# Seven half-depth block products instead of eight in three chunks of a feed-forward

## The chip, the core and the metric

The kernel runs on one core of a Trainium2 chip. The core has a matrix unit (TensorE, PE in the profile, with its weight loads as PEld), VectorE (DVE), ScalarE (ACT), GpSimd (POOL), a queue engine that only starts transfers (SyncE, SP), an on-chip memory of 128 partitions (SBUF) and eight banks of accumulators (PSUM), each 128 x 512 float32. The metric is device time in microseconds, the median of several runs.

## The reference

One block of a streaming encoder on x (256 rows x 2048), all in float32:

```python
h = modulate(rms_norm(x, ffn1_pre_g[l]), sh1, sc1)
y = swiglu(h, ffn1_w_gu[l], ffn1_w_down[l])
x = x + 0.5 * gt1 * rms_norm(y, ffn1_post_g[l])
...
x = x + gt2 * rms_norm(y, mix_post_g[l])
h = modulate(rms_norm(x, ffn2_pre_g[l]), sh3, sc3)
y = swiglu(h, ffn2_w_gu[l], ffn2_w_down[l])
x = x + 0.5 * gt3 * rms_norm(y, ffn2_post_g[l])
```

where `swiglu(h, w_gu, w_down)` is `(silu(h @ G) * (h @ U)) @ w_down`, with G and U the two halves of w_gu, each 2048 x 5504. Between the two feed-forwards lie an in-projection, attention, a spatial gate and an out-projection. The modulation vectors (sh, sc, gt) are a product of silu(c) with a 2048 x 18432 matrix. The change touches the gate and up products of the second feed-forward.

## The kernel before

**Products.** A float32 product is made of three matmuls: every operand is split into a high part (rounded to the matrix unit's type) and a low part (the rest), and `mm3` (L111) multiplies high by high, high by low and low by high into one bank. Weights arrive by transfers of 1 MB into `raw` tiles (three buffers, `load`, L117), and `split` (L152) makes the parts, 1024 columns at a time: ScalarE copies to the high part (L155), VectorE subtracts (L156). The parts go to buffers that `slot` (L143) takes from a repeating sequence of pools; in the second feed-forward these are 3 of `wx3` and 4 of `wsp`, seven pairs in all.

**The feed-forward** (`ffn`, L324). The 5504 columns form eleven chunks: ten of 512 and a last one of 384. `visit` (L342) loads the weights of two k-tiles (gate and up of each), splits them, and does, for two k-tiles, gate and up, and two row tiles of x, one `mm3` each: 24 matmuls of 128 x 512. Eight visits make a chunk, on four PSUM banks from the pool `pmm` (six banks; `ptr` has the other two). `act` (L395) then does silu(gate) on ScalarE and the product with up on VectorE. `trans` (L411) turns the result so that it can be a weight of the next product, half a chunk later, through `ptr`. When two chunks are ready and a third has been computed, `down` (L430) multiplies the two by their rows of w_down: for each of four column blocks two loads, 48 matmuls into two banks, then an addition to y (L453). The last chunk has `down_last` (L455), which also does the norm and the result.

In the second feed-forward the chunks go in order 0 to 10 (L583). Chunk 0 has its own form (`lead_chunk`, L356). The downs come after chunks 2, 4, 6, 8 and 10, for the pairs 0 and 1, 2 and 3, 4 and 5, 6 and 7, 8 and 9.

**Order.** The code is written in program order; a scheduler places the instructions on the engines at compile time and may move one ahead where its operands are ready, and each engine then executes its own list in order. SP issues all weight loads in one list. A load waits there until its buffer is free, and the loads behind it wait too.

**Modulation blocks.** The modulation matrix is worked off in the background: `tick` (L223), called at each visit, adds a rate to a counter and, whenever that passes one, issues `ada_block` (L198), a load of 1 MB into a two-buffer pool `adap` and a 2048-wide multiply-and-sum on VectorE (L202). It also runs one step of the list `later`, if there is one. `flush_ada` (L234) issues what is left of a vector, `gate` (L239) makes the row of gt that the norm needs.

**Around the second feed-forward.** x after mixing (`x2`) is made by `post` (L309), `pre` (L271) turns it into h for the feed-forward, and `finish3` (L1049) adds the result to `x2` and stores it. `x2` stays in SBUF from one to the other. `rstd` (L173) uses a small power on GpSimd (L178).

Of the kernel before, what the change touches and what calls it, by code (L numbers as in the profile page):

```python
# [18 lines left out]
P = 128  # L19
# [10 lines left out]
CHUNKS = [(c, min(CH, FF - c)) for c in range(0, FF, CH)]  # L30
MAX_REL = 128
# [31 lines left out]
def block_kernel(ctx: ExitStack, tc: tile.TileContext, a: dict, out: bass.AP):  # L63
# [21 lines left out]
    x_dram = dr.tile([S, D], F32, tag="x1", name="x1")  # L85
    xp = ctx.enter_context(tc.tile_pool(name="xp", bufs=1))
# [30 lines left out]
    def load(src, off, n):  # L117
        raw = wraw.tile([P, 2048], F32, tag="raw", name=nm("raw"))
        nc.sync.dma_start(raw[:, :n], src[off:off + P * n].rearrange("(p n) -> p n", p=P))
        return raw  # L120
# [203 lines left out]
    def ffn(wgu, wdn, h, avp, ahp, plan, rate, gate_of, finish, lead=(), after_lead=(), ahead=None):  # L324

        hi, lo = h
        C = len(CHUNKS)
# [10 lines left out]
        def gu_load(c, p):  # L338
            off, w = CHUNKS[c]
            return load(wgu, 2 * D * off + p * P * 4 * w, 4 * w)  # L340
# [53 lines left out]

        def act(c):  # L395
            w = CHUNKS[c][1]
            res = []
            for t in range(NT):
                gu = [ps_of[c][b][t][:, :w] for b in range(2)]
                if c in acc:  # L400
                    for b in range(2):
                        nc.vector.tensor_tensor(acc[c][b][t], acc[c][b][t], gu[b], op=ALU.add)
                    gu = [acc[c][b][t] for b in range(2)]
                av = avp.tile([P, CH], F32, tag="av", name=nm("av"), bufs=2)
                nc.scalar.activation(av[:, :w], gu[0], AF.Silu)
                nc.vector.tensor_tensor(av[:, :w], av[:, :w], gu[1], op=ALU.mult)
                res.append(av)
            act_of[c] = res
            del ps_of[c]
# [20 lines left out]
        def down(cs):  # L430
            fresh = not y
            if fresh:
                y.extend(yp.tile([P, D], F32, tag=f"y{t}", name=nm(f"y{t}")) for t in range(NT))
            for n in range(4):
                ns = slice(n * CH, (n + 1) * CH)
                ps = [pmm.tile([P, CH], F32, tag="mm", name=nm("dn")) for _ in range(NT)]
                for c in cs:
                    off, w = CHUNKS[c]
# [145 lines left out]
        tick_acc[1] = rate if plan else 0.0  # L584
        for c in todo:
            if plan and c not in acc and slots["hold"] is not None:
                use_slots((wsp, 4), (slots["hold"], 3))
                slots["hold"] = None
            p0 = max(p for d, p, _ in plan if d == c) + 1 if c in acc else 0
            pm, pe = (p0 + KT // 2) // 2, KT // 2  # L590
            if lead and c == 0:
                lead_chunk(0, lead)
                use_slots(*after_lead)
                p0 = pe
            else:
                ps_of[c] = banks()
            for p in range(p0, pe):
                if p == pm:
# [3 lines left out]
                visit(c, p, p == p0, p == pe - 1)  # L602
            act(c)
            tick_acc[1] = rate
            if c == C - 1:
                g = gate_of()
                tick_acc[1] = 0.0
            if len(ready) == 2:
                down(ready)
# [368 lines left out]
    with tc.tile_pool(name="gp2", bufs=1) as gp:  # L978
# [47 lines left out]
        with tc.high_priority():  # L1026
            for t in range(NT):
                for b in range(2):
                    r = evac_b(t, 2 + b, ps[b][t])
                pre(2, x2, t, post(x2, t, y, r), h3)  # L1030
    mxs.close()
# [3 lines left out]
    with ExitStack() as ahs:  # L1035
# [8 lines left out]

        def gate3():
            flush_ada(GT[2])
            return gate(2, 0.5, gp)

        def finish3(t, y, r):  # L1049
            for j in range(4):  # L1050
                js = slice(j * CH, (j + 1) * CH)
                nc.vector.scalar_tensor_tensor(out=x2[t][:, js], in0=y[t][:, js], scalar=r, in1=x2[t][:, js], op0=ALU.mult, op1=ALU.add)
                nc.sync.dma_start(out[t * P:(t + 1) * P, js], x2[t][:, js])

        ffn(a["w_gu2"], a["w_dn2"], h3, avp, ahp, None, 0.15, gate3, finish3, lead=lead,
            after_lead=((wx3, 3), (wsp, 4)))
# [7 lines left out]
def _gu(w):  # L1064
    g, u = w[:, :FF].reshape(KT, P, FF), w[:, FF:].reshape(KT, P, FF)
    units = []
    for c, n in CHUNKS:
# [64 lines left out]
```

## Time and profile before

| | us |
|---|---|
| median of 3 runs | 1838.58 |
| lowest, highest | 1838.19, 1840.62 |
| the profiled execution | 1839.32 |
| its span, first to last instruction | 1837.2 |

| engine | busy us | share of the span |
|---|---|---|
| PE | 1803.2 | 98% |
| PEld | 1501.1 | 82% |
| DVE | 1328.4 | 72% |
| ACT | 854.5 | 47% |
| POOL | 31.3 | 2% |

The profile is that of one execution. Its page shows the span in 40 slices of some 46 us, with each engine's busy share in tenths; the second feed-forward is in the last 16 of them. Further views group the instructions by line, list them in order of time, list who waited for whom, or give the busy time of each engine in a chosen stretch. Matmuls overlap in the matrix unit, so one lasts longer than the distance to the next, and a busy share of 100% says that there is no hole, not how fast the work goes.

### The profile page before, as it was taken

The numbers are of one execution on the slowest core, as the hardware profiler recorded it, in microseconds if no ns is written. First come the engines' busy times: TensorE is split into PE (matmuls) and PEld (weight loads), VectorE is DVE, ScalarE is ACT, GpSimd is POOL, SyncE is SP. The second block draws the span as 40 slices with busy tenths as digits, with TensorE's granted clock in tenths as the row PEclk, the third lists the DMA queues.
The fourth block names the chain that finished last, engine by engine and source line by source line (L and its number), as shares of the span: only waits on it lengthen the run. The fifth ranks groups of instructions, "written<-read, shape, count | busy, mean of one in ns | idle before, by whom it ended". The sixth has DMA issues, their size and how long they took to land.

```text
span 1837.2 us, 21286 instructions
## 1 busy us (share of the span) xinstructions
PE 1803.2 (98%) x8271; PEld 1501.1 (82%) x8271; DVE 1328.4 (72%) x1481; ACT 854.5 (47%) x1105; POOL 31.3 (2%) x59
## 2 busy tenths in 40 slices
PE   7999999999999999999999999999999999999997
PEld 6777788888888898788888887888888888888896
DVE  7989998988877876768789986774445445445456
ACT  6544354444443344645555557444443443443342
POOL 0000000000000000000001000000000000000000
PEclk9999999999999999999999999999999999999999
DMA  9988788898888876479788974875555555555461
GB/s 395 385 335 318 286 320 342 326 367 332 336 335 321 329 289 261 172 276 358 292 307 326 382 291 165 332 305 187 195 191 187 196 191 187 196 190 186 160 250 70
DMA packets 71477, 499.11 MB, mean 272 GB/s; under 512 B 7968, under 2 KB 8144, under 8 KB 13136
## 3 DMA queue, kind: packets, MB, share of 16 engines
q1 hardware_dynamic: 70560, 492.48, 70.2%
q0 software_dynamic: 720, 5.24, 0.7%
q8 instruction: 65, 1.06, 0.2%
q14 instruction: 36, 0.29, 0.0%
q10 hardware_dynamic: 96, 0.02, 0.0%
HBM read 493.50 MB, written 4.22 MB: 271 GB/s over the span
## 4 chain that ended last, share of the span: by engine, by line
PE 93%; DVE 4%; ACT 1%; issue 1%; DMA 0%; POOL 0%; POOLq 0%; DVEq 0%; SPq 0%; ACTq 0%
PE gu L114 16%; PE gu L115 16%; PE gu L113 16%; PE dn L113 8%; PE dn L114 8%; PE dn L115 8%; PE pj L113 4%; PE pj L115 4%; PE pj L114 4%; PE wo L113 1%; PE wo L115 1%; PE wo L114 1%; DVE lo L156 1%; PE atp L418 1%; PE xtp L281 1%
## 5 line engine op out<-in xcount | busy, mean ns | idle before, releaser
L155 ACT CAST hi<-raw 128x1024 fp32r<-128x1024 f32 (+1 forms) x628 | 645.9, 1042 | 811.5 <-PE gu L115 422.6
L156 DVE TENSOR_TENSOR lo<-raw,hi 128x1024 fp32r<-128x1024 f32 (+1 forms) x628 | 747.8, 1208 | 380.9 <-ACT hi L155 379.5
L113 PE MATMUL gu<-hi,hhi 128*128 128x512 f32 (+1 forms) x1396 | 536.8, 387 | 8.9 <-DVE acc L392 4.2
L114 PE MATMUL gu<-lo,hhi 128*128 128x512 f32 (+1 forms) x1396 | 537.9, 385 | 0.4 <-DVE lo L156 0.3
L115 PE MATMUL gu<-hi,hlo 128*128 128x512 f32 (+1 forms) x1396 | 537.7, 385 | 0.0
L202 DVE CUSTOM_DVE_ANT_0 ada<-ada,c_bc,small 128x2048 f32<-128x2048 f32 x144 | 337.4, 2344 | 9.6 <-PE qkt L797 9.0
L113 PEld LDWEIGHTS gu<-hi,hhi 128*128 128x128 f32 x1396 | 262.4, 188 | 62.4 <-ACT hi L155 5.2
L114 PEld LDWEIGHTS gu<-lo,hhi 128*128 128x128 f32 x1396 | 263.0, 188 | 50.3 <-DVE lo L156 1.2
L115 PEld LDWEIGHTS gu<-hi,hlo 128*128 128x128 f32 x1396 | 262.9, 188 | 50.0
L113 PE MATMUL dn<-hi,ah 128*128 128x512 f32 x640 | 249.2, 389 | 0.0
L114 PE MATMUL dn<-lo,ah 128*128 128x512 f32 x640 | 249.0, 389 | 0.0
L115 PE MATMUL dn<-hi,al 128*128 128x512 f32 x640 | 249.0, 389 | 0.0
L113 PEld LDWEIGHTS dn<-hi,ah 128*128 128x128 f32 x640 | 120.1, 188 | 25.1
L115 PEld LDWEIGHTS dn<-hi,al 128*128 128x128 f32 x640 | 120.1, 188 | 25.0
L114 PEld LDWEIGHTS dn<-lo,ah 128*128 128x128 f32 x640 | 120.2, 188 | 24.8
L113 PE MATMUL pj<-hi,hhi 128*128 128x512 f32 x304 | 120.9, 398 | 0.0
L114 PE MATMUL pj<-lo,hhi 128*128 128x512 f32 x304 | 120.4, 396 | 0.0
L115 PE MATMUL pj<-hi,hlo 128*128 128x512 f32 x304 | 120.1, 395 | 0.0
L115 PEld LDWEIGHTS pj<-hi,hlo 128*128 128x128 f32 x304 | 57.1, 188 | 11.1
L114 PEld LDWEIGHTS pj<-lo,hhi 128*128 128x128 f32 x304 | 57.4, 189 | 10.7
L113 PEld LDWEIGHTS pj<-hi,hhi 128*128 128x128 f32 x304 | 57.4, 189 | 10.6
L453 DVE TENSOR_TENSOR y<-y,dn 128x512 f32<-128x512 f32 x64 | 41.9, 682 | 17.5 <-PE dn L115 17.5
(167 smaller groups left out, 1071.8 us busy)
## 6 DMA issues: line engine op xcount, KB each, us to landing
raw<-in_w_gu_dram SPq DMA_DIRECT2D x158, 1024.0 KB, 4.8
ada<-in_w_ada_dram SPq DMA_DIRECT2D x144, 1024.0 KB, 7.0
raw<-in_w_dn_dram SPq DMA_DIRECT2D x86, 1024.0 KB, 4.8
raw<-in_w_in_dram SPq DMA_DIRECT2D x40, 1024.0 KB, 6.2
raw<-in_w_out_dram SPq DMA_DIRECT2D x16, 1024.0 KB, 7.3
raw<-in_w_gu_dram SPq DMA_DIRECT2D x16, 768.0 KB, 5.3
x<-in_x_dram SPq DMA_DIRECT2D x4, 1024.0 KB, 7.5
gate<-gd POOLq DMA_DIRECT2D x3, 1024.0 KB, 8.4
```

The lines of the kernel that those rows point to most:

```text
L113: nc.tensor.matmul(ps, ah, wh, start=start, stop=False)
L114: nc.tensor.matmul(ps, ah, wl, start=False, stop=False)
L115: nc.tensor.matmul(ps, al, wh, start=False, stop=stop)
L155: i_hi = nc.scalar.copy(hi[:, :n], raw)
L156: i_lo = nc.vector.tensor_tensor(lo[:, :n], raw, hi[:, :n].bitcast(F32), op=ALU.subtract)
L202: inst = nc.vector.tensor_tensor_reduce(out=st, in0=st, in1=c_bc, scale=1.0, scalar=bada[:, i:i + 1], op0=ALU.mult, op1=ALU.add, accum_out ...
L281: nc.tensor.matmul(ps[:, q, :], x[t][:, (4 * j + q) * P:(4 * j + q + 1) * P], dg, start=True, stop=True)
L418: nc.tensor.transpose(ps[:, q, :], av[:, q * P:(q + 1) * P], ident)
L453: nc.vector.tensor_tensor(y[t][:, ns], y[t][:, ns], ps[t], op=ALU.add)
```

## The change

Write h as blocks of 128 rows by 1024 (half the depth), and the weights of a chunk as blocks of 1024 by 512: gate and up, upper and lower half. Then gate and up of both row tiles are a 2 x 2 by 2 x 2 block product, eight block products of half the depth. For the chunks 5, 7 and 9 (`FAST`) the new code forms the same four results out of seven, from sums and differences of blocks on both sides:

- `sum_steps` makes four combinations of the blocks of h, once, before they are needed: two sums that put high and low parts together again, four differences, and their split into parts. They run as steps of `later` during the first down. The results lie in tiles that were those of `x2`, of the broadcast c vector and of the gate row.
- `fast_visit` loads the blocks of one k-tile of a half into a tile of `adap` (four blocks in part 0, three in part 1), adds blocks to each other in place on VectorE (three additions in part 0, one in part 1), splits all of them, and does one `mm3` for each: 12 matmuls in part 0, 9 in part 1. Eight visits make a part.
- Part 0 of chunk c+1 is done between the visits of the down that follows chunk c, one before each. It takes four banks of `pmm`; that down therefore uses `ptr` for every second column block. `first_sums` combines its four results.
- Part 1 is done in the next ordinary chunk, two visits each behind its visits 1 to 4, on three more banks. `second_sums` combines these with the first ones and does the activation. `trans` of the chunk comes behind visit 6, that of the chunk before it moves from visit 4 to visit 1.
- `x2` is stored to DRAM by GpSimd's queue after mixing and loaded again (`x3`) at the last chunk.
- The rate of the modulation blocks in the second feed-forward goes from 0.15 to 0.77.
- The host lays out the weights of the three chunks in the order in which the new visits read them.

```diff
+FAST = (5, 7, 9)
+HK = KT // 2
+def gu_offsets(fast):
+    res, off = [], 0
+    for c, (_, n) in enumerate(CHUNKS):
+        res.append(off)
+        off += HK * P * (2048 + 1536) if c in fast else 2 * D * n
+    return res
...
+    x2_dram = dr.tile([S, D], F32, tag="x2", name="x2")
...
-    def load(src, off, n):
-        raw = wraw.tile([P, 2048], F32, tag="raw", name=nm("raw"))
+    def load(src, off, n, raw=None):
+        if raw is None:
+            raw = wraw.tile([P, 2048], F32, tag="raw", name=nm("raw"))
         nc.sync.dma_start(raw[:, :n], src[off:off + P * n].rearrange("(p n) -> p n", p=P))
...
+        def multiply(gus):
+            res = []
+            for g, u in gus:
+                av = avp.tile([P, CH], F32, tag="av", name=nm("av"), bufs=2)
+                nc.scalar.activation(av, g, AF.Silu)
+                nc.vector.tensor_tensor(av, av, u, op=ALU.mult)
+                res.append(av)
+            return res
+        a_hl = {}
+        def sum_steps():
+            r = []
+            def rows(t):
+                r.append(adap.tile([P, KT, P], F32, tag="ada", name=nm("asum")))
+                ts = slice(t * P, (t + 1) * P)
+                nc.vector.tensor_tensor(r[t], hi[:, :, ts].bitcast(F32), lo[:, :, ts].bitcast(F32), op=ALU.add)
+            def minus(o, a, b):
+                o, a, b = (r[t][:, HK * i:HK * (i + 1), :] for t, i in (o, a, b))
+                nc.vector.tensor_tensor(o, a, b, op=ALU.subtract)
+            def to_hl(t):
+                tiles = sum_tiles(t)
+                for i in range(2):
+                    ks = slice(HK * i, HK * (i + 1))
+                    split_act(r[t][:, ks, :], tiles[0][:, ks, :], tiles[1][:, ks, :])
+                for i, name in enumerate((("a3", "a7"), ("a6", "a1"))[t]):
+                    a_hl[name] = [v[:, HK * i:HK * (i + 1), :] for v in tiles]
+            return [lambda: rows(0), lambda: rows(1),
+                    lambda: minus((0, 0), (0, 1), (0, 0)), lambda: minus((0, 1), (0, 1), (1, 1)),
+                    lambda: minus((1, 1), (1, 1), (0, 0)), lambda: minus((1, 0), (1, 0), (1, 1)),
+                    lambda: to_hl(0), lambda: to_hl(1)]
+        def first_banks():
+            return [pmm.tile([P, CH], F32, tag="mm", name=nm("m")) for _ in range(4)]
+        def second_banks():
+            return [pmm.tile([P, CH], F32, tag="mm", name=nm("m")) for _ in range(2)] + \
+                   [ptr.tile([P, CH], F32, tag="tr", name=nm("m"))]
+        def fast_visit(c, part, p, ps):
+            n = (2048, 1536)[part]
+            raw = load(wgu, offs[c] + part * HK * P * 2048 + p * P * n, n,
+                       adap.tile([P, D], F32, tag="ada", name=nm("raw")))
+            blk = [raw[:, i * CH:(i + 1) * CH] for i in range(n // CH)]
+            sums = ((1, 0), (2, 1), (3, 2)) if part == 0 else ((2, 0),)
+            for i, j in sums:
+                nc.vector.tensor_tensor(blk[i], blk[i], blk[j], op=ALU.add)
+            sp = [split(raw[:, o:min(o + 1024, n)]) for o in range(0, n, 1024)]
+            a = lambda name: [v[:, p, :] for v in a_hl[name]]
+            if part == 0:
+                sts = [a("a3"), hst(p, 0), a("a1"), a("a7")]
+            else:
+                sts = [hst(p, 1), hst(p + HK, 1), a("a6")]
+            for i, st in enumerate(sts):
+                s = slice((i % 2) * CH, (i % 2 + 1) * CH)
+                mm3(ps[i], st, (sp[i // 2][0][:, s], sp[i // 2][1][:, s]), p == 0, p == HK - 1)
+        def spare(i):
+            return sm.tile([P, CH], F32, tag=("xn", "h32")[i], name=nm("cs"), bufs=2)
+        def first_sums(ps):
+            m3, m5, m1, m7 = ps
+            t1, t2, t3 = spare(0), spare(0), spare(1)
+            nc.scalar.copy(t1, m1)
+            nc.scalar.copy(t2, m5)
+            nc.vector.tensor_tensor(t3, t2, m3, op=ALU.add)
+            nc.vector.tensor_tensor(t2, t1, t2, op=ALU.subtract)
+            nc.vector.tensor_tensor(t1, t1, m3, op=ALU.add)
+            nc.vector.tensor_tensor(t2, t2, m7, op=ALU.add)
+            return t1, t2, t3
+        def second_sums(c, ts, ps):
+            m2, m4, m6 = ps
+            t1, t2, t3 = ts
+            t4 = spare(1)
+            nc.scalar.copy(t4, m2)
+            nc.vector.tensor_tensor(t2, t2, m4, op=ALU.add)
+            nc.vector.tensor_tensor(t1, t1, t4, op=ALU.subtract)
+            nc.vector.tensor_tensor(t4, t4, m4, op=ALU.add)
+            nc.vector.tensor_tensor(t1, t1, m6, op=ALU.add)
+            act_of[c] = multiply([(t2, t3), (t4, t1)])
...
-        def down(cs):
-            fresh = not y
+        def down(cs, fill=()):
+            fill = list(fill)
+            fresh, fast_on = not y, bool(fill)
             if fresh:
                 y.extend(yp.tile([P, D], F32, tag=f"y{t}", name=nm(f"y{t}")) for t in range(NT))
             for n in range(4):
                 ns = slice(n * CH, (n + 1) * CH)
-                ps = [pmm.tile([P, CH], F32, tag="mm", name=nm("dn")) for _ in range(NT)]
+                pool, tag = (ptr, "tr") if fast_on and n % 2 else (pmm, "mm")
+                ps = [pool.tile([P, CH], F32, tag=tag, name=nm("dn")) for _ in range(NT)]
                 for c in cs:
+                    if fill:
+                        fill.pop(0)()
...
+        seven = {}
         for c in todo:
+            if c in fast:
+                continue
             if plan and c not in acc and slots["hold"] is not None:
                 use_slots((wsp, 4), (slots["hold"], 3))
                 slots["hold"] = None
...
                 p0 = pe
             else:
                 ps_of[c] = banks()
+            second = c - 1 in fast
             for p in range(p0, pe):
-                if p == pm:
+                if p == (p0 + 1 if second else pm):
                     for r in ready:
                         if r not in stat:
                             trans(r)
                 visit(c, p, p == p0, p == pe - 1)
+                if second and 1 <= p <= 4:
+                    if p == 1:
+                        mb = second_banks()
+                    for i in range(2):
+                        fast_visit(c - 1, 1, 2 * (p - 1) + i, mb)
+                    if p == 4:
+                        second_sums(c - 1, seven.pop(c - 1), mb)
+                        ready.append(c - 1)
+                if second and p == pe - 2:
+                    trans(c - 1)
             act(c)
             tick_acc[1] = rate
+            if fast and c == 2:
+                later.extend(sum_steps())
             if c == C - 1:
                 g = gate_of()
                 tick_acc[1] = 0.0
             if len(ready) == 2:
-                down(ready)
+                if c + 1 in fast:
+                    ma = first_banks()
+                    down(ready, [lambda p=p: fast_visit(c + 1, 0, p, ma) for p in range(HK)])
+                    seven[c + 1] = first_sums(ma)
+                else:
+                    down(ready)
                 ready = []
...
+                nc.gpsimd.dma_start(x2_dram[t * P:(t + 1) * P, :], x2[t])
...
+        def sum_tiles(t):
+            flush_ada(GT[2])
+            pools = (((xp, "x0"), (xp, "x1")), ((const, "c_bc"), (gp, "gate")))[t]
+            return [p.tile([P, KT, P], F32R, tag=tag, name=nm("ahl")) for p, tag in pools]
+        x3 = []
         def gate3():
             flush_ada(GT[2])
+            x3.extend(load_x(x2_dram, nc.gpsimd))
...
-        ffn(a["w_gu2"], a["w_dn2"], h3, avp, ahp, None, 0.15, gate3, finish3, lead=lead,
-            after_lead=((wx3, 3), (wsp, 4)))
+                nc.vector.scalar_tensor_tensor(out=x3[t][:, js], in0=y[t][:, js], scalar=r, in1=x3[t][:, js], op0=ALU.mult, op1=ALU.add)
+                nc.sync.dma_start(out[t * P:(t + 1) * P, js], x3[t][:, js])
+        ffn(a["w_gu2"], a["w_dn2"], h3, avp, ahp, None, 0.77, gate3, finish3, lead=lead,
+            after_lead=((wx3, 3), (wsp, 4)), fast=FAST, sum_tiles=sum_tiles)
...
+    for i, (c, n) in enumerate(CHUNKS):
+        if i in fast:
+            b = lambda v, k: v[k, :, c:c + n]
+            units += [np.stack([b(u, k + HK), b(u, k), b(g, k), b(g, k + HK)], axis=1) for k in range(HK)]
+            units += [np.stack([b(g, k), b(g, k + HK), b(u, k)], axis=1) for k in range(HK)]
+            continue
```

More of the change, by code (lines that the diff above doesn't have):

```diff
@@ L322, in block_kernel, with ffn @@
     LEAD = 8
-    def ffn(wgu, wdn, h, avp, ahp, plan, rate, gate_of, finish, lead=(), after_lead=(), ahead=None):
+    def ffn(wgu, wdn, h, avp, ahp, plan, rate, gate_of, finish, lead=(), after_lead=(), ahead=None,
+            fast=(), sum_tiles=None):
         hi, lo = h
+        offs = gu_offsets(fast)
         C = len(CHUNKS)
@@ L338, in gu_load @@
         def gu_load(c, p):
-            off, w = CHUNKS[c]
-            return load(wgu, 2 * D * off + p * P * 4 * w, 4 * w)
+            w = CHUNKS[c][1]
+            return load(wgu, offs[c] + p * P * 4 * w, 4 * w)
         def visit(c, p, start, stop, bank_outer=False, raw=None, qs=(0, 1), sp=None):
@@ L1051, in finish3, with _gu @@
                 js = slice(j * CH, (j + 1) * CH)
-                nc.vector.scalar_tensor_tensor(out=x2[t][:, js], in0=y[t][:, js], scalar=r, in1=x2[t][:, js], op0=ALU.mult, op1=ALU.add)
-                nc.sync.dma_start(out[t * P:(t + 1) * P, js], x2[t][:, js])
-        ffn(a["w_gu2"], a["w_dn2"], h3, avp, ahp, None, 0.15, gate3, finish3, lead=lead,
-            after_lead=((wx3, 3), (wsp, 4)))
+                nc.vector.scalar_tensor_tensor(out=x3[t][:, js], in0=y[t][:, js], scalar=r, in1=x3[t][:, js], op0=ALU.mult, op1=ALU.add)
+                nc.sync.dma_start(out[t * P:(t + 1) * P, js], x3[t][:, js])
+        ffn(a["w_gu2"], a["w_dn2"], h3, avp, ahp, None, 0.77, gate3, finish3, lead=lead,
+            after_lead=((wx3, 3), (wsp, 4)), fast=FAST, sum_tiles=sum_tiles)
 def _flat(units):
     return np.concatenate([np.ascontiguousarray(u).reshape(-1) for u in units])
-def _gu(w):
+def _gu(w, fast=()):
     g, u = w[:, :FF].reshape(KT, P, FF), w[:, FF:].reshape(KT, P, FF)
     units = []
-    for c, n in CHUNKS:
+    for i, (c, n) in enumerate(CHUNKS):
[4 more added lines that the diff above has]
+            continue
         for k in range(0, KT, 2):
@@ L1117 @@
         "w_out": _flat(_pairs(w["w_out"][0], (0, 8), ((0, 1), (2, 3))) + _pairs(w["w_out"][0], (8, 16), ((0, 1), (2, 3)))),
-        "w_gu2": _gu(w["ffn2_w_gu"][0]),
+        "w_gu2": _gu(w["ffn2_w_gu"][0], FAST),
         "w_dn2": _down(w["ffn2_w_down"][0]),
```

## The prediction

> **What bounds the kernel now.** I read the page first, then the windows of the second feed-forward, the waits in them, and single timelines for durations. The change lies wholly in that last stage, but for two stores just before it.
>
> ```profile
> span 1837.2 us, 21286 instructions
> ...
> PE 1803.2 (98%) x8271; PEld 1501.1 (82%) x8271; DVE 1328.4 (72%) x1481; ACT 854.5 (47%) x1105; POOL 31.3 (2%) x59
> ...
> PE   7999999999999999999999999999999999999997
> ...
> DVE  7989998988877876768789986774445445445456
> ...
> PEclk9999999999999999999999999999999999999999
> ```
>
> The reader is to see that the matrix unit (PE) has no hole between the first and the last slice, that its clock is full throughout, and that VectorE (DVE), at 8 to 9 tenths in the first feed-forward, falls to 4 or 5 in the second. A busy PE may still be one that runs slowly, so I ask for its rate next: the windows, with the columns PE, PEld, DVE, ACT, POOL, clock, DMA share and GB/s.
>
> ```profile
> 1377.10:1420.60 43.50, 43.50 (x193) 36.02 (x192) 24.38 (x24) 17.84 (x19) 0.00 (x0) 1.00 0.54 193
> 1420.60:1465.03 44.43, 44.43 (x202) 36.88 (x201) 22.00 (x20) 17.86 (x19) 0.00 (x0) 1.00 0.52 189
> 1377.10:1509.46 132.36, 132.36 (x594) 109.77 (x593) 68.37 (x64) 54.54 (x57) 0.00 (x0) 1.00 0.53 191
> ```
>
> The cuts are the moments at which ScalarE starts the activation of a finished chunk:
>
> ```profile
> 1332.67 1.08 ACT L405 ACTIVATE av<-gu 128x512 f32<-128x512 f32 x2
> 1377.10 1.08 ACT L405 ACTIVATE av<-gu 128x512 f32<-128x512 f32 x2
> ...
> 1465.03 1.08 ACT L405 ACTIVATE av<-gu 128x512 f32<-128x512 f32 x2
> 1509.46 1.08 ACT L405 ACTIVATE av<-gu 128x512 f32<-128x512 f32 x2
> ```
>
> From 1332.67 to 1377.10 is one gate/up chunk: 16 k-tiles x 2 row tiles x 2 (gate, up) x 3 = 192 matmuls, with 8 small transposes, 44.43 us. From 1377.10 to 1465.03 is one such chunk and one down product of 4 x 2 x 24 = 192 matmuls: 87.93 us. The difference, 43.50 us, is 192 matmuls alone: **0.2266 us for one 128x512 matmul**; the transposes take the other 0.93 us. The round repeats (132.36 us = two chunks and one down).
>
> ```profile
> DVE lo L156 <- ACT hi L155: 65.5, 49, 1.5
> ACT hi L155 <- PE gu L115: 52.9, 33, 1.7
> ACT hi L155 <- PE dn L115: 26.6, 16, 1.7
> ```
>
> These are all the waits of that round. ScalarE waits for PE to give back a split buffer, VectorE waits for ScalarE, PE waits for nobody. So PE's instruction count sets the time, and a removed matmul is worth its whole spacing as long as that stays so.
>
> **The change, part by part.** *PE.* A fast chunk has 7 products x 8 k-tiles x 3 = 168 matmuls of the same shape in place of 192. Three chunks: 72 fewer, 72 x 0.2266 = **16.3 us**. Down, transposes and the other eight chunks keep their counts. In the Trainium skill, "TensorE: Matmul & The Clock Gate", section "Back-to-back issue gap", gives about 131 ns for a sustained N=512 matmul beside its weight load, by which the 72 would be worth an estimated 9.4 us, and the end 1830.7 with the same 1.5 us of hand-overs as below. The 0.2266 us measured here with a weight load in front of every matmul speak against it, and they decide.
>
> *VectorE.* Durations, in a run from the timeline and single from the groups (mean ns of one), with ScalarE's conversion:
>
> ```profile
> 331.85 3.49 DVE L156 TENSOR_TENSOR lo<-raw,hi 128x1024 fp32r<-128x1024 f32 x3
> ...
> 1389.26 1.28 DVE L453 TENSOR_TENSOR y<-y,dn 128x512 f32<-128x512 f32 x2
> ...
> L156 DVE TENSOR_TENSOR lo<-raw,hi 128x1024 fp32r<-128x1024 f32 x176 | 215.6, 1225 | 231.2 <-ACT hi L155 231.2
> L155 ACT CAST hi<-raw 128x1024 fp32r<-128x1024 f32 x176 | 185.6, 1055 | 279.5 <-PE gu L115 174.6 <-PE dn L115 104.9
> ...
> L303 DVE TENSOR_TENSOR y<-y,gate 128x512 f32<-128x512 f32 x8 | 5.5, 686 | 2.4 <-ACT junk L171 2.4
> ```
>
> In a run, one 1024-wide operation follows another after (3.49-1.23)/2 = 1.13 us, a 512-wide after 1.28-0.68 = 0.60; alone they last 1.22 and 0.69. Part 0 of a fast chunk adds 8 visits of 3 weight sums and 2 splits: 8 x (3 x 0.60 + 2 x 1.13) = 32.5 us, to the 24.4 us that the first window above already has. PE's time for both is 43.5 + 8 x 12 x 0.2266 = 65.3 us, so VectorE is 56.9/65.3 = **87% busy**. The sums form a chain (each reads the one before). No row shows a chained 512-wide pair back to back; taken as good as free it costs 0.60 a sum, at most its whole 0.69. That gives 59.1 us, 91%.
>
> Part 1 lies between visits 1 to 4 of the next chunk: 8 x (0.60 + 1.13 + 0.60) = 18.6 us, with four sums of products before it and six operations behind it (10 x 0.60 = 6 us), on 22.0 us; PE has 44.4 + 8 x 9 x 0.2266 = 60.7 us. That is 77%. Two windows of the first feed-forward bear on whether PE keeps its pace beside so busy a VectorE:
>
> ```profile
> 427.71:515.66 87.95, 87.95 (x393) 72.93 (x392) 72.02 (x69) 35.29 (x36) 0.00 (x0) 1.00 0.84 332
> 240.00:360.00 120.00, 120.00 (x546) 99.38 (x546) 107.82 (x114) 58.30 (x70) 0.00 (x0) 1.00 0.85 326
> 180.00:220.00 40.00, 37.16 (x162) 29.84 (x161) 37.09 (x45) 15.83 (x18) 0.00 (x0) 1.00 0.77 295
> ```
>
> The first is again one down and one chunk, and takes 87.95 us, just what it takes in the second feed-forward (87.93), with VectorE at 82% and 332 GB/s. The second shows no hole at 90%; the third, at 93%, loses 7%. So 87% should be covered, not by much. Seven split buffers (3 + 4) stand between the splits and PE: in a part 0 window two of four hold 12 matmuls and two hold 6, on average 2.0 us, an estimated lead of 14 us, which also swallows a wait inside one visit.
>
> *ScalarE* gets 8 x 2 conversions of about 1.05 us more in part 0: 17.8 + 17 = 35 of 65 us, hidden by PE. *Making the summed inputs* (two 2048-wide sums, estimated at 2.2 us from the step between 0.60 and 1.13; four 1024-wide differences, four splits) is 2 x 2.2 + 8 x 1.13 = 13.4 us of VectorE in the first down product, which has room (24.4 of 43.5 us busy in a like window). The higher rate of the remaining modulation blocks moves VectorE work inside the same slack. Both cost nothing; if that cover were gone, PE would wait for one of them, 2.2 us.
>
> *Transfers.* A fast chunk reads 8 x 1024 KB and 8 x 768 KB instead of 8 x 1024 KB, all issued by SP in one queue with the others.
>
> ```profile
> raw<-in_w_gu_dram SPq DMA_DIRECT2D x158, 1024.0 KB, 4.8
> ada<-in_w_ada_dram SPq DMA_DIRECT2D x144, 1024.0 KB, 7.0
> ...
> raw<-in_w_gu_dram SPq DMA_DIRECT2D x16, 768.0 KB, 5.3
> ```
>
> Part 0 moves 16 MB-sized loads in 65.3 us, 257 GB/s; the windows above carry 332. Its raw tiles come from the two-buffer pool. A buffer is held for a landing (4.8 to 7.0 us), three sums (2.1), a conversion (1.05) and two splits (2.4): 10 to 13 us, against 2 x 8.2 us that PE spends on two pairs of visits. It fits. In part 1, landing 5.3 + 0.7 + 1.05 + 1.9 = 9.0 us against one group of 42 matmuls, 9.5 us: it fits barely, and SP stands in front of the next chunk's load while it waits; the lead covers four such groups.
>
> *New waits.* Part 0 takes two banks from the activation that frees them, whose second half on VectorE is
>
> ```profile
> 1378.38 1.28 DVE L406 TENSOR_TENSOR av<-av,gu 128x512 f32<-128x512 f32 x2
> ```
>
> The gate banks go after ScalarE's Silu (1.08 us for both); six matmuls on the two free banks (1.36 us) stand before their use, so the wait should be nothing. If they waited for the whole activation (1377.10 to 1379.66, 2.56 us) it would be 1.2 us, three times. Behind that wait stands PE alone, and nobody else waits for it. The next chunk's up banks wait for two copies of product banks (2 x 0.6 us), behind 24 matmuls of down: nothing, or up to 2.2 us if VectorE's four sums came first. Ends: 0 and 3 x 3.4 = 10 us; less than nothing is excluded, as PE had no idle time there to win. I take 0.5 us a chunk, **1.5 us**, near the end that today's hand-overs (no idle) show.
>
> *Round trip of x.* Two 1 MB stores and two loads on POOL's queue:
>
> ```profile
> 1103.39 0.55 POOL L178 TENSOR_TENSOR r<-ms,mhalf 128x1 f32<-128x1 f32 x1 [4.67 <-DVE ms L176]
> 1106.99 0.93 POOL L178 TENSOR_TENSOR r<-ms,mhalf 128x1 f32<-128x1 f32 x1 [3.05 <-DVE ms L176]
> ...
> L91 POOL DMA_DIRECT2D x<-x x2 | 1.1, 574 | 23.9 <-ACT hi L155 23.9
> ```
>
> An issue holds POOL 0.57 us, and POOL stands idle 3.05 us between the two small powers that the path waits for: nothing, at most 0.6 us. The loads have the last down product before them.
>
> Sum on the profiled execution: 1839.3 (span 1837.2 and 2.1 around it) - 16.3 + 1.5 = 1824.5; that execution lies 0.7 us above the median of 1838.6, so **1823.8**.
>
> **Rivals.** *VectorE falls behind in part 0.* If every operation there costs its single duration, as a chain with a flush after each would, the window is 16 x 1.22 + 10 x 0.69 + 8 x (3 x 0.69 + 2 x 1.22) = 62.5 us, 96%, past the 93% of 180:220. Priced by that window's loss, 7.1% of 3 x 65.3 us is 13.9 us, less what the lead swallows: 4 to 14 us on the saving, 1826 to 1836, about 1831. For it: the sum chain. Against: the 1.13 and 0.60 us spacings. The Trainium skill, "VectorE: DVE Perf Modes", section "The DRAIN you can't avoid", says that after each operation the pipe is flushed before the next may start, and that one which is not held starts earlier; by the flush the single durations are the spacing, as in this rival. The rows in a run agree with the second half for independent operations; for chained sums no run here shows it.
>
> *The two-buffer ring paces part 1.* If landings take 7.0 us there, a group takes 10.7 us, not 9.5: 4 x 1.2 = 4.8 us a chunk, which the lead of 14 us covers; what is left of it, 1824 to 1828, lies in my main case.
>
> *The saving is eaten.* The upper price of the first, 14 us, with 1.5 to 5 us of hand-overs: 1838 to 1841.
>
> *Slower.* The instruction order is fixed at compile time. If in it each low-part split of a down-and-fast pair stands right behind its own conversion, nothing overlapping, VectorE's pair costs 4 x (1.05 + 1.22) + 3 x 0.69 + 0.69 = 11.8 us against PE's 8.2. Eight pairs lose 29.4, less 14 of lead: 15.4 us a chunk, 46 in all, 1868. It decides from about 10.6 us a pair, where a chunk loses its 5.4. Against it: three splits in a run at 331.85.
>
> **Numbers.** Main case (1821 to 1828) 0.61; VectorE behind (1828 to 1834.9) 0.19; eaten 0.09; slower 0.11. About 0.2% (3.7 us) is what a measurement here can tell from no change. The range runs from 1821 (all 16.3 us and a microsecond of order elsewhere) to 1835, which leaves out the last two cases. Faster 0.80, same 0.09, slower 0.11.
>
> **What would show it.** Right: a round of 126.9 us instead of 132.4 between activations, 168 matmuls a fast chunk at 0.2266 us, VectorE 85 to 92% in the three part 0 windows, waits still ending at PE, no PE idle over 1 us at the hand-overs. Wrong: PE waiting on a low split or a raw landing in those windows, chained sums over 0.7 us apart, PE idle before the next chunk's first up matmul, or a matmul spacing that grows.

## The result and the profile after

| | before | after |
|---|---|---|
| median, us | 1839.04 (4 runs, one more than above, 1838.19 to 1840.62) | 1825.41 (4 runs, 1823.84 to 1826.15) |
| the profiled execution | 1839.32 | 1825.13 |
| its span | 1837.2 | 1823.4 |

The ratio is 0.9924, 95% interval 0.9907 to 0.9941: 13.6 us faster where 14.8 were forecast. The spans differ by 13.8 us. The first lines of the page after, as shown of before:

```profile
span 1823.4 us, 21523 instructions
...
PE 1789.1 (98%) x8199; PEld 1487.7 (82%) x8199; DVE 1455.0 (80%) x1659; ACT 902.0 (49%) x1166; POOL 33.5 (2%) x63
...
PE   7999999999999999999999999999999999999997
...
DVE  6989997988778876858789987787447788788766
...
PEclk9999999999999999999999999999999999999999
```

PE has 8271 - 8199 = 72 matmuls less and still no hole; VectorE's last slices went from 4 and 5 tenths to 6 to 8. The activations of the ordinary chunks cut the second feed-forward into rounds (timeline of after, ScalarE):

```profile
1377.55 1.08 ACT L521 ACTIVATE av<-gu 128x512 f32<-128x512 f32 x2
1505.21 1.07 ACT L521 ACTIVATE av<-gu 128x512 f32<-128x512 f32 x2
1632.83 1.07 ACT L521 ACTIVATE av<-gu 128x512 f32<-128x512 f32 x2
1750.97 0.86 ACT L521 ACTIVATE av<-gu 128x384 f32<-128x384 f32 x2
```

A round takes 127.66 us where it took 132.36, and 126.92 were forecast (132.36 - 24 x 0.2266). The first row is 0.45 us later than the same activation of before (1377.10): that much lies ahead of the first fast chunk (whether the change costs it is taken up at the end of the point-by-point account). The windows of after, part 0 first (activation to the end of the down), then part 1, then two stretches of 40 us:

```profile
1377.55:1444.83 67.28, 67.28 (x297) 55.36 (x296) 56.96 (x63) 35.25 (x37) 0.00 (x0) 1.00 0.69 243
1505.21:1572.44 67.23, 67.23 (x297) 55.30 (x295) 58.53 (x66) 35.25 (x37) 0.00 (x0) 1.00 0.68 243
1632.83:1700.05 67.22, 67.22 (x296) 55.29 (x295) 58.31 (x67) 34.38 (x37) 1.11 (x2) 1.00 0.66 237
1444.83:1505.21 60.38, 60.38 (x275) 49.95 (x274) 47.60 (x56) 33.86 (x39) 0.00 (x0) 1.00 0.70 253
...
1500.00:1540.00 40.00, 40.00 (x181) 33.04 (x180) 37.15 (x44) 21.09 (x23) 0.00 (x0) 1.00 0.71 264
1620.00:1660.00 40.00, 40.00 (x182) 33.05 (x181) 37.76 (x45) 21.55 (x24) 0.00 (x0) 1.00 0.70 259
```

PE is busy in every microsecond of them, beside a VectorE that is at 85 to 87% in part 0, 79% in part 1, and 93 and 94% over 40 us. PE's waits from 1370 to 1800 us are one row:

```profile
PE dn L135 <- ACT aw L540: 0.2, 1, 0.2
```

It belongs to the last chunk's down product, and before has the same wait of 0.2 us there.

So 16.3 us of matmuls were removed and 13.8 us came, without a wait to explain the rest. Of the 2.5 us that are missing 0.45 lie ahead of the first fast chunk. The others must lie in the pace of PE itself, which a busy share doesn't show. The timeline of after, four matmuls of one part 0 visit:

```profile
1388.47 0.40 PE L137 MATMUL m<-hi,hlo 128*128 128x512 f32 x1
1388.70 0.39 PE L135 MATMUL m<-hi,ahl 128*128 128x512 f32 x1
1388.93 0.40 PE L136 MATMUL m<-lo,ahl 128*128 128x512 f32 x1
1389.17 0.40 PE L137 MATMUL m<-hi,ahl 128*128 128x512 f32 x1
```

Starts lie 0.23 us apart, some 0.24, where they were 0.2266. The same from the trace's start times in ns, for the twelve matmuls of a part 0 visit and the four of the down behind them (median over the 24 visits, which agree within 1 ns). `a3`, `h`, `a1`, `a7` name the stationary operand (three matmuls each):

```
        a3 a3 a3  h  h   h  a1  a1  a1  a7  a7  a7  dn  dn  dn  dn
after  227 227 227 227 227 235 233 233 236 224 231 236 228 232 231 227
```

Ten spacings in a row are off, nine longer and one shorter, by 53 ns in all in a visit; a pair of part 1 visits has 66 ns more. 24 x 0.053 + 12 x 0.066 = **2.1 us**, and 0.45 + 2.1 is the missing 2.5 of these two executions.

### The profile page after: what moved, and what is told of

It is laid out like the page before. It is cut to its first block, busy times and chain, and to the rows that moved or that the text cites. A ratio compares the mean times of both kernels' runs of the same rounds, so it can differ in the third digit from the quotient of the medians.

```text
span 1823.4 us, 21523 instructions
## 1 busy us (share of the span) xinstructions
PE 1789.1 (98%) x8199; PEld 1487.7 (82%) x8199; DVE 1455.0 (80%) x1659; ACT 902.0 (49%) x1166; POOL 33.5 (2%) x63
## 4 chain that ended last, share of the span: by engine, by line
PE 92%; DVE 3%; issue 3%; ACT 1%; DMA 0%; POOL 0%; POOLq 0%; DVEq 0%; SPq 0%; ACTq 0%
PE gu L137 14%; PE gu L136 14%; PE gu L135 14%; PE dn L135 8%; PE dn L136 8%; PE dn L137 8%; PE pj L135 4%; PE pj L137 4%; PE pj L136 4%; PE m L137 2%; PE m L136 2%; PE m L135 2%; PE wo L135 1%; PE wo L137 1%; PE wo L136 1%
## 5 line engine op out<-in xcount | busy, mean ns | idle before, releaser
L178 ACT CAST hi<-raw 128x1024 fp32r<-128x1024 f32 (+2 forms) x676 | 685.3, 1028 | 743.2 <-PE gu L137 301.9
L179 DVE TENSOR_TENSOR lo<-raw,hi 128x1024 fp32r<-128x1024 f32 (+2 forms) x676 | 788.1, 1190 | 205.5 <-ACT hi L178 202.5
L135 PE MATMUL gu<-hi,hhi 128*128 128x512 f32 (+1 forms) x1204 | 461.9, 387 | 8.8 <-DVE acc L417 4.2
L136 PE MATMUL gu<-lo,hhi 128*128 128x512 f32 (+1 forms) x1204 | 463.4, 385 | 0.4 <-DVE lo L179 0.3
L137 PE MATMUL gu<-hi,hlo 128*128 128x512 f32 (+1 forms) x1204 | 463.3, 385 | 0.0
L135 PEld LDWEIGHTS gu<-hi,hhi 128*128 128x128 f32 x1204 | 226.1, 188 | 54.9 <-ACT hi L178 5.2
L136 PEld LDWEIGHTS gu<-lo,hhi 128*128 128x128 f32 x1204 | 227.1, 189 | 43.3 <-DVE lo L179 1.2
L137 PEld LDWEIGHTS gu<-hi,hlo 128*128 128x128 f32 x1204 | 226.9, 188 | 42.6
L474 DVE TENSOR_TENSOR raw<-raw 128x512 f32<-128x512 f32 x96 | 66.2, 690 | 33.7 <-DMA raw<-in_w_gu_dram 32.4
```

Of the source, the lines that this page charges most:

```text
L135: nc.tensor.matmul(ps, ah, wh, start=start, stop=False)
L136: nc.tensor.matmul(ps, ah, wl, start=False, stop=False)
L137: nc.tensor.matmul(ps, al, wh, start=False, stop=stop)
L178: i_hi = nc.scalar.copy(hi[:, :n], raw)
L179: i_lo = nc.vector.tensor_tensor(lo[:, :n], raw, hi[:, :n].bitcast(F32), op=ALU.subtract)
L474: nc.vector.tensor_tensor(blk[i], blk[i], blk[j], op=ALU.add)
```

## The experiments

Three theories for the slow stretch. **A**: splits come twice as densely to PE as in an ordinary visit (two per 12 matmuls, not two per 24). **B**: something of the stationary operand, since the stretch begins one spacing before `a1` is first multiplied. **C**: VectorE's weight sums, or its load, disturb PE's reads.

**Other order in a visit.** `a1` and `a7` first; in part 1 `a6` first.

```diff
-            for i, st in enumerate(sts):
+            for i in ((2, 3, 0, 1), (2, 0, 1))[part]:
+                st = sts[i]
```

> Same products, but those on the second split of a visit come first, so that PE meets one new split behind 12 (part 0) or 9 (part 1) matmuls instead of two. Theory A (a fresh split every 6 matmuls slows the matrix unit: 0.233 us from the sixth matmul of every fast visit on): the slow stretch of part 0 goes, spacing 0.2267 us all through, 0.053 us a visit in part 0 (24 visits) and up to 0.066 us a pair in part 1 (12 pairs): 1.3 to 2.1 us less than the changed kernel, about 1823.5 us. Theory B (the stationary tiles made from sums lie badly): the slow stretch moves to the front of the visit with those tiles, time unchanged, 1825.4. Theory C (VectorE and ScalarE traffic): unchanged in place and time.

1825.41 us (ratio 0.9928, 0.9912 to 0.9945), the time of after. The same numbers moved with `a1`: 235 now stands one spacing before the visit, 233, 233, 236, 224, 231 ... at its start, and its last three are at 227. The place in the visit and the split that feeds it don't count; the stretch goes with `a1`.

**Dense splits without the change.** The kernel before with four splits of 512 columns in each visit of chunks 3, 5 and 7.

```diff
+                if not plan and c in (3, 5, 7):
+                    parts = [split(raw[:, i * w:(i + 1) * w]) for i in range(4)]
```

> The kernel before, with the visits of chunks 3, 5 and 7 of the second feed-forward split in four pieces of 512 columns instead of two of 1024: no fast product, but a fresh split every 6 matmuls. Theory A: the spacing in these 24 visits rises to 0.230 to 0.233 us for most of their matmuls, 24 x 24 x about 0.005 = 2 to 3 us more than before, 1841 to 1842. Theories B and C: the spacing stays at 0.2267, time 1838 to 1840.

1840.30 us in one execution; before gave 1837.95 to 1840.22 on that chip. Its timeline, around chunk 3 and the down beside it:

```profile
1246.16 1.07 ACT L411 ACTIVATE av<-gu 128x512 f32<-128x512 f32 x2
1334.05 1.08 ACT L411 ACTIVATE av<-gu 128x512 f32<-128x512 f32 x2
```

87.89 us, as before (87.93). What makes this execution longer stands ahead of chunk 3: the first row lies 1.37 us later than in before (1244.79), and the span is 1838.5 for 1837.2. A falls.

**No weight sums.**

```diff
-            for i, j in sums:
-                nc.vector.tensor_tensor(blk[i], blk[i], blk[j], op=ALU.add)
```

> The changed kernel without the additions of weight blocks (left out: the sums, so the products are of other weights); 96 VectorE operations less, 22 us a chunk. If VectorE is covered: time within 0.5 us of the changed kernel, spacing of the fast matmuls as before (0.235, 0.233, ...). Theory C: the slow stretch becomes shorter or goes, up to 2 us less. If the chain of sums held PE anywhere: up to 2 us less too, with PE idle gone.

1826.19 us in one execution; the round is 127.66 us as in after (1378.62 to 1506.28), the spacings are the same to the nanosecond. VectorE's busy time in it is 87.48 us for 104.56, so neither the 96 sums nor the load that they make cost PE anything, and C falls.

**Stationary operands from h alone.**

```diff
-                sts = [a("a3"), hst(p, 0), a("a1"), a("a7")]
+                sts = [hst(p, 0), hst(p, 1), hst(p + HK, 0), hst(p + HK, 1)]
...
-                sts = [hst(p, 1), hst(p + HK, 1), a("a6")]
+                sts = [hst(p, 1), hst(p + HK, 1), hst(p, 0)]
```

> The changed kernel with every stationary operand of the fast products taken from h instead of its sums (changed: the combinations of h, so the result is another function). Theory B: no slow stretch, about 2 us less, 1823.4. Theories A and C: the same spacing pattern, 0.235 us from the sixth matmul on, time 1825 to 1826.

1823.70 us in one execution, every spacing 226 or 227 ns. Its window over the first round:

```profile
1378.06:1505.03 126.97, 126.97 (x570) 105.31 (x569) 104.75 (x118) 69.14 (x77) 0.00 (x0) 1.00 0.68 247
```

That is the forecast round (126.92) with the same work on VectorE (104.75 us; after has 104.56). B holds: the stationary tiles cost the 2.1 us. The stretch begins with `a1` in part 0 and `a6` in part 1. `sum_steps` puts just these two into one pair of tiles: their high parts into `c_bc` (byte 17632 of each partition in the compiled program), their low parts into the gate row's tile (204544). `a3`, at 227 ns, lies in the former tiles of `x2` (159488 and 167680), and so does `a7`, which comes right behind `a1`; the parts of h lie at 43520 and 59904.

**Where the tile lies.** Two readings of B: `c_bc` is slow because 17632 isn't a multiple of 64 (B1 in the expectations), or because it lies low in the partition (B3). First, `c_bc` moved to 16512, a multiple of 64; then the parts exchanged.

```diff
+    c_bc = const.tile([P, D], F32, tag="c_bc", name="c_bc")
     small = const.tile([P, KT + 9 * KT + V_N], F32, tag="small", name="small")
```

> The changed kernel with one tile moved: the c vector's tile, which later holds the high parts of the combinations that the slow products use, is allocated ahead of the small constants, so that it starts at a multiple of 64 bytes instead of 32 bytes past one; no instruction differs. Theory B1 (a weight load from a tile that starts 32 bytes past a multiple of 64 is slower): the slow stretch is gone, all fast matmuls 0.2267 us apart, 2.1 us less, about 1823.4. Theory B2 (these tiles are slow for another reason, as where they lie, who wrote them, or which pair they form): the pattern 0.235, 0.233, ... stays, 1825.4.

1826.07 us in one execution; the stretch got worse, 80 ns a visit in place of 53 (232, 241, 240, 235, 233, 236 ...), the round 128.00 us. A multiple of 64 does not take the stretch away.

```diff
-            pools = (((xp, "x0"), (xp, "x1")), ((const, "c_bc"), (gp, "gate")))[t]
+            pools = (((xp, "x0"), (xp, "x1")), ((gp, "gate"), (const, "c_bc")))[t]
```

> The changed kernel with the two tiles of that pair exchanged: the low parts lie in the tile 32 bytes past a multiple of 64, the high parts in the other. A high part is loaded twice in three matmuls, a low part once. Theory B1: a shorter or shallower stretch that begins two matmuls later, about half the excess (0.025 to 0.03 us instead of 0.053 a visit of part 0), about 1 us less. Theory B2: no change if the pair is at fault, or no stretch at all if only what is loaded twice matters.

1823.11 us in one execution, below the lowest run of after (1823.84). Only two spacings of a visit are still long (235, 232), 14 ns in all:

```profile
1376.82:1504.00 127.18, 127.18 (x570) 105.34 (x569) 103.69 (x117) 69.01 (x77) 0.00 (x0) 1.00 0.70 245
```

So `c_bc` is the slow tile. A high part is loaded for two of three matmuls, a low part for one; the loss a visit fell to about a quarter, further than to the half which that ratio would give.

**Controls.** `c_bc` and `ident` placed first, both at multiples of 64, in the kernel before and in after.

```diff
+    c_bc = const.tile([P, D], F32, tag="c_bc", name="c_bc")
+    ident = const.tile([P, P], F32, tag="ident", name="ident")
     small = const.tile([P, KT + 9 * KT + V_N], F32, tag="small", name="small")
```

> The kernel before with the c vector's tile and the identity's tile both ahead of the small constants, so that both start at multiples of 64 bytes. The identity is an operand of every transposition. Theory B1: the ten or so matmuls behind each group of transpositions, 0.23 us apart today, go back to 0.2267; 458 matmuls of the trace of before are 229 to 240 ns apart, at 6 ns each up to 2.7 us less, 1836 to 1838. Theory B2: the same time, 1838.5.

> The changed kernel with both tiles moved as in the run before. Theory B1: the 2.1 us of the slow stretches and what the kernel before wins there: 1821 to 1823.4, and against the kernel before with the same two tiles moved the full 72 x 0.2267 = 16.3 us within the scatter. Theory B2: 1825.4.

Before so changed: 1838.34 us beside 1838.67 (ratio 0.9999, 0.9989 to 1.0009). After so changed: 1825.89 us (0.9933, 0.9918 to 0.9948), with the spacings of the first move. In neither does the time gain by it. One thing moved in the trace of before so changed: in the chunks without a down, the long spacings behind the transposes are two (233 231) where they were six off their pace (224 231 236 228 232 231), 0.01 us a chunk.

**Higher up.** The pool of `c_bc` behind that of y, so that `c_bc` lies at 34016.

```diff
-    const = ctx.enter_context(tc.tile_pool(name="const", bufs=1))
     yp = ctx.enter_context(tc.tile_pool(name="yp", bufs=1))
+    const = ctx.enter_context(tc.tile_pool(name="const", bufs=1))
```

> The changed kernel with the pool of constants (among them the tile of the slow high parts and the identity) allocated behind the two tiles of y instead of ahead of them: its tiles start 16384 bytes higher in each partition, at 32896 and above, with the same offsets to multiples of 64. No instruction differs otherwise. Theory B3 (weight loads from the lowest part of a partition, below some 26 KB, are slower): no slow stretch, 2.1 us less in the fast visits and some of the 2.7 us behind transpositions: 1821 to 1823.5. Theory B4 (it depends on which tiles follow each other, or on the offset within 64 or 128 bytes): the pattern stays, 1825.4 to 1826.

1825.40 us (0.9927, 0.9910 to 0.9943); the spacings are those of after. If the place counts, 34016 is as bad as 17632; the limit that I had set for the low part is wrong. Both lie 32 bytes past a multiple of 64 and give 53 ns, 16512 is a multiple and gives 80, so the offset may shape the pattern though it doesn't make it.

**h itself in the low part.** The kernel before with the pool of h in front: high parts at 16512, low parts at 32896.

```diff
+    hp = ctx.enter_context(tc.tile_pool(name="hp", bufs=1))
     const = ctx.enter_context(tc.tile_pool(name="const", bufs=1))
     yp = ctx.enter_context(tc.tile_pool(name="yp", bufs=1))
-    hp = ctx.enter_context(tc.tile_pool(name="hp", bufs=1))
```

> The kernel before with the tiles of h allocated first: the high parts lie at 16512 to 32896 in each partition, the low parts behind them; the constants move up. The high part of h is loaded twice in three matmuls of every gate, up and in-projection product. Theory B3: these some 5100 matmuls go from 0.2267 to 0.232 us or more, 25 to 40 us more than before, 1864 to 1879. Theory B4: within 2 us of 1838.5.

1863.37 us in one execution, beside 1838.20: **25 us slower** with not one operation changed. Its activations:

```profile
1349.31 1.08 ACT L405 ACTIVATE av<-gu 128x512 f32<-128x512 f32 x2
1394.91 1.08 ACT L405 ACTIVATE av<-gu 128x512 f32<-128x512 f32 x2
1483.99 1.08 ACT L405 ACTIVATE av<-gu 128x512 f32<-128x512 f32 x2
1529.58 1.08 ACT L405 ACTIVATE av<-gu 128x512 f32<-128x512 f32 x2
```

A chunk takes 45.60 us where it took 44.43; with a down 89.08 where it took 87.93. Only the chunk's 192 matmuls became slower, by 1.17/192 = 6 ns each; those of the down, whose stationary tiles stayed, did not. PE waits for nobody there, and a weight load is still written at 188 ns. The constants and y moved up with the change, but these 192 matmuls read neither. The place of the stationary tile changes the matmul's spacing; the offset within 64 or 128 bytes does not explain it, as 16512 and 43520 are both multiples of 128.

What it is about the place stays open. With high parts at 16512, 17632 and 34016 the matmuls are slow, at 43520 and above 159000 fast; whether 32896, where only low parts lay, is slow by itself, no run shows. A part of h fills 16384 bytes of a partition, 1024 for each k-tile. The mean spacing in ns of the twelve matmuls of each k-tile, worked out from the start times of one chunk in each (up to 1377.10 in before, up to 1394.91 here; the transposes stand ahead of k-tile 8):

```
k-tile  0 to 7     8      9   10 to 15
before   226.7  235.4  227.6   226.7
here     233.3  239.6  232.9   231.7 to 232.8
```

All are fast in the one and slow in the other, though both tiles pass through every address modulo 16384. So a rule on the address modulo 16384, by which 17632 and 34016 are equal, is out. A plain border between 34016 and 43520 has this against it: the low parts of k-tiles 11 to 15 lie above 43520 here, and nothing changes there. For high parts alone a border would have to lie between 42208, where `c_bc` ended in the run before, slow in all its visits, and 43520; no run tests that.

Nor is the place all that counts. In the next chunk here (up to 1483.99) it is k-tiles 0 to 7 that have 231.7 to 232.9 ns and k-tiles 9 to 15 that have 233.3: the pace changes behind the transposes, not at an address. And the six spacings behind `a1`'s last in after, 224 231 236 228 232 231, also follow the transposes in before, where no tile in `c_bc` is multiplied; that tail is not peculiar to the tile.

**How far VectorE's cover reaches.** Four more 512-wide additions in each part 0 visit: does the lead in the buffers swallow them, or does every fast chunk pay for them?

```diff
+            for i in range(4 if part == 0 else 0):
+                nc.vector.tensor_tensor(blk[3], blk[3], blk[0], op=ALU.add if i % 2 else ALU.subtract)
```

> The changed kernel with four more 512-wide additions and subtractions of the same block in each visit of part 0 (two pairs that cancel up to rounding): 32 more VectorE operations in each part 0 window, 0.60 to 0.73 us each, 78 to 82 us of VectorE in 67.3 us of PE. Theory with a lead (seven split buffers hold some 14 us of PE work, and part 1 and the plain visits refill them): PE loses at most 1 us a chunk, 1825 to 1829. Theory without (PE follows VectorE as soon as it is over 93% busy, as in the window 180:220 of before): 11 to 15 us a chunk, 1858 to 1870.

1843.47 us in one execution, 18 us above after: neither of the two. Its activations:

```profile
1378.23 1.08 ACT L523 ACTIVATE av<-gu 128x512 f32<-128x512 f32 x2
1506.88 1.22 ACT L523 ACTIVATE av<-gu 128x512 f32<-128x512 f32 x2
1642.63 1.28 ACT L523 ACTIVATE av<-gu 128x512 f32<-128x512 f32 x2 [0.81 <-PE gu L137]
1768.33 0.88 ACT L523 ACTIVATE av<-gu 128x384 f32<-128x384 f32 x2
```

The rounds are 128.65, 135.75 and 125.70 us, those of after 127.66, 127.62 and 118.14: 1.0, 8.1 and 7.6 us more. Its windows show the end of the second part 0 and what follows:

```profile
1500.00:1540.00 40.00, 39.44 (x177) 32.18 (x177) 38.66 (x51) 18.03 (x20) 0.00 (x0) 1.00 0.59 224
1540.00:1580.00 40.00, 35.68 (x145) 27.47 (x144) 39.19 (x49) 18.75 (x19) 0.00 (x0) 0.96 0.53 196
1580.00:1620.00 40.00, 40.00 (x182) 33.03 (x181) 32.17 (x39) 22.52 (x27) 0.00 (x0) 1.00 0.75 268
```

The 32 additions at 0.687 us are 22 us on the 57 of a part 0 window of 67.3: 11.7 us too many. The first round loses 1.0 of them, so a lead of some 10.7 us (worked out, not seen directly) stood in the buffers, somewhat below the estimate of 14. It isn't won back in time: the later rounds lose 8, with VectorE at 98% and 36 matmuls missing from 40 us. The lead is a stock, filled by the plain chunks, and what follows a part 0 refills about 4 us of it (11.7 less 8, worked out).

**Four fast chunks.** Chunk 3 too, the sums of h one chunk earlier, the modulation blocks faster so that they are done by then, and the two tiles exchanged as above.

```diff
-FAST = (5, 7, 9)
+FAST = (3, 5, 7, 9)
...
-            if fast and c == 2:
+            if fast and c == 1:
...
-            pools = (((xp, "x0"), (xp, "x1")), ((const, "c_bc"), (gp, "gate")))[t]
+            pools = (((xp, "x0"), (xp, "x1")), ((gp, "gate"), (const, "c_bc")))[t]
...
-        ffn(a["w_gu2"], a["w_dn2"], h3, avp, ahp, None, 0.77, gate3, finish3, lead=lead,
+        ffn(a["w_gu2"], a["w_dn2"], h3, avp, ahp, None, 1.75, gate3, finish3, lead=lead,
```

> The changed kernel with chunk 3 formed by seven products too (four chunks: 3, 5, 7, 9), the high parts of the summed inputs of rows 1 in the gate's tile instead of the tile in the low part of the partition, the summed inputs made one chunk earlier (behind chunk 1) and the remaining modulation blocks dealt out at 1.75 a visit so that they are done by then. Counted from the 1839.0 us of before: 4 x 24 matmuls x 0.2266 = 21.8 us off; the slow stretch that is left 4 x (8 x 0.014 + 4 x 0.02) = 0.8 us back, 0.3 us for the stores of x: 1818.3. If both gains hold: 1817 to 1820, a round of 127.2 us between activations with no PE idle in it. If a fast chunk's VectorE work must be prepaid by the plain chunks ahead of it (the lead as a stock, which the four extra sums a visit used up in the first round), the fourth chunk in a row has less, and VectorE is also filled by the modulation blocks in chunks 1 and 2: PE would wait on high or low parts in the first fast chunk, 2 to 6 us, 1820 to 1825. If the placing of the high parts was worth nothing in itself: 1820 and the spacing of 232 to 236 ns back in the fast visits.

1822.18 us (1820.49 to 1825.20; ratio 0.9904, 0.9887 to 0.9920): the fastest of the kernels here by its median, though the interval overlaps that of after. Its profiled execution is the slowest of its four, so what it shows as lost needn't be lost in the others. The rounds are as forecast:

```profile
1251.91 1.08 ACT L521 ACTIVATE av<-gu 128x512 f32<-128x512 f32 x2
1379.05 1.07 ACT L521 ACTIVATE av<-gu 128x512 f32<-128x512 f32 x2
```

127.14 us (127.2 forecast), and the next two 127.13 each, without a wait. The loss is ahead of them; PE's waits from 1160 to 1252 us:

```profile
PE gu L135 <- ACT hi L178: 1.5, 1, 1.5
PE gu L136 <- DVE lo L179: 1.2, 3, 0.5
PE atp L534 <- DVE av L522: 0.6, 1, 0.6
```

They all lie between 1204 and 1216 us, where VectorE's list holds the sums of h (2.3 us each), a modulation block and the splits of PE's weights one behind the other (timeline):

```profile
1204.70 2.29 DVE L440 TENSOR_TENSOR asum<-hhi,hlo 128x2048 f32<-128x2048 f32 x1
...
1209.24 2.35 DVE L225 CUSTOM_DVE_ANT_0 ada<-ada,c_bc,small 128x2048 f32<-128x2048 f32 x1
...
1212.65 2.28 DVE L440 TENSOR_TENSOR asum<-hhi,hlo 128x2048 f32<-128x2048 f32 x1
```

Chunk 2 takes 49.58 us (1202.33 to 1251.91) where it took 44.48. Of these 5.1 us the three rows have 3.3; by the start times of the matmuls nearly all of it lies between 1203.95 and 1216.5. The rival named the right price, 2 to 6 us, and the wrong place: not the first fast chunk, whose lead was full.

## Why the prediction was right, point by point

The mechanism was right: PE's count of matmuls sets the time, and 72 matmuls fewer are worth nearly their spacing.

| term, us | forecast | measured |
|---|---|---|
| 72 matmuls at 0.2266 | -16.3 | -16.3 (8199 in place of 8271) |
| hand-overs | +1.5 | 0 |
| fast matmuls at another spacing | 0 | +2.1 |
| ahead of the first fast chunk | 0 | +0.45 (within the scatter) |
| sum | -14.8 | -13.8 |

*PE.* The step that was mis-sized reads "168 matmuls of the same shape in place of 192 ... 72 x 0.2266": it took the shape for all that sets the spacing. With the stationary operands of h the round is 126.97 us, with `c_bc` as one of them 127.66. "A matmul spacing that grows" stood among the signs of being wrong, at no price. By the Trainium skill, "TensorE: Matmul & The Clock Gate", section "Back-to-back issue gap", 131 ns a matmul would have given an estimated saving of 9.4 us; the measured 13.8, and the spacing of 226 to 227 ns with operands from h alone, decide against it here.

*Hand-overs.* The 1.5 us were not there: six and 24 matmuls in front of the shared banks were cover enough, and the one wait of 0.2 us at the last chunk stands in before too. This error has the other sign than the spacing's: that the sum came within 1.0 us, with one term off by 1.5 and another by 2.1, is luck.

*VectorE.* Forecast 87% and 77%, measured 85 to 87% and 79%. The chained sums were mis-sized (timeline of after):

```profile
1384.35 2.14 DVE L474 TENSOR_TENSOR raw<-raw 128x512 f32<-128x512 f32 x3
```

With 0.69 for a single one, (2.14 - 0.69)/2 = 0.725 us from one to the next, beyond the end of 0.69 that I had called "at most". Among the signs of being wrong stood "chained sums over 0.7 us apart"; this sign appeared, and PE lost nothing by it. The Trainium skill, "VectorE: DVE Perf Modes", section "The DRAIN you can't avoid", has the next operation wait for the pipe to empty; the spacing of the chained sums, a little more than a single's duration, agrees with that, though no run separates it from the wait of one sum for the result of the one before. It cost nothing, as the kernel without sums shows: the rival "VectorE behind" was right that a chain gains nothing over single operations, and wrong on the window (62.5 us forecast, 57.0 to 58.5 measured) and on what follows for PE. The 93% window of before that lost 7% was no rule either: after has 94% over 40 us with PE full.

*Transfers.* The two-buffer ring held up VectorE, not PE. Waits of the first round in after:

```profile
DVE raw L474 <- DMA raw<-in_w_gu_dram: 13.6, 11, 2.0
DVE lo L179 <- ACT hi L178: 9.4, 16, 1.5
```

VectorE stood 11 times for a raw tile, 2.0 us at most, five of them in part 0, of which I had said "It fits"; the lead swallowed it.

*Ahead of the first fast chunk* I had put the stores of x at nothing, at most 0.6 us. The 0.45 us between the two profiled executions show no cost. At the last down matmul of the first feed-forward, which the change does not touch, after already is 0.52 us later (746.14 for 745.62). And the activation at which after has 1377.55 lies anywhere from 1376.82 to 1378.62 in the kernels above that differ from after only in the fast products or in the place of their operands. What the stores cost, if anything, is not shown.

## What to carry to other kernels

Where matmuls follow each other without a hole, compare their start times, not the busy share: that stays at 100% when each takes 3% longer; it was 2.1 us here, and 25 us when all of h lay in the wrong place. Before reusing a free tile as a stationary operand, compare the spacing there with that of another tile, and give the better place to the part that is loaded twice. A lead in buffers is a stock: work that fits into it once must also fit into the rate at which it is refilled.

## What was not expected of the hardware

The spacing of a 128x512 matmul with its weight load in front depends on where the stationary tile lies in the partition: 226.6 ns from tiles at byte 43520 and above, on average 232.7 ns (45.60 us less 0.93 for the transposes, over 192) with h's high parts at 16512 and its low parts at 32896. What about the place does it stays open. With high parts in `c_bc` alone the longer spacings begin one matmul ahead of the tile's first use and go on for six behind its last, the same six that follow the transposes in before; with low parts there, two spacings are longer. The records of the weight loads keep their 188 ns; the starts of the matmuls show it, and a little their records, at 395 to 396 ns for 389 to 390 with h in the low place.
